# Moving a substitution tile's clears and eleven weight remainders from GpSimd to VectorE in a hybrid decoder step

## The chip, the cores and the metric

The kernel runs on one core of a Trainium2 chip. The metric is the device time of one execution in microseconds (us); the median of three runs is given. Five engines of the core work beside each other, each through its own instructions in a fixed order: TensorE (PE in the profile, with its weight loads as PEld), VectorE (DVE), ScalarE (ACT), GpSimd (POOL) and SyncE (SP), which issues the transfers.

## The reference

One inference step of a hybrid decoder layer for 2048 prompt tokens and 8 x 8 sample tokens, model width 1024. Cut to what matters here:

```python
h = _rmsnorm(x, norm_mix_w[i]) * (1 + sc1) + sh1
proj = jnp.einsum('bld,de->ble', h, w_in[i])
qkv, z, b_raw, a_raw, sq, sk, sv = _split_cols(proj, IN_SPLITS)
o_dn, n_dn_buf, n_S = _deltanet_mixer(qkv, z, b_raw, a_raw, ...)   # 4 heads, chunks of 64
o_swa, n_k, n_v = _swa_prompt(sq, sk, sv, swa_sinks[i], rel_bias)  # window 128
mix = jnp.concatenate([o_dn, o_swa], axis=-1)
x = x + g1 * jnp.einsum('ble,ed->bld', mix, w_out[i])
h = _rmsnorm(x, norm_ffn_w[i]) * (1 + sc2) + sh2
u = jnp.einsum('bld,df->blf', h, ffn_w_up[i])
gate, up = jnp.split(u_c + ffn_conv_b[i], 2, axis=-1)              # u_c: causal convolution of u
x = x + g2 * jnp.einsum('blf,fd->bld', jax.nn.silu(gate) * up, ffn_w_down[i])
```

In each chunk the DeltaNet mixer needs the inverse of a unit lower triangular matrix:

```python
A = jnp.where(strict, bc[..., :, None] * kk * decay, 0.0)
T = lax.linalg.triangular_solve(A + eye, jnp.broadcast_to(eye, A.shape),
                                left_side=True, lower=True, unit_diagonal=True)
```

## The kernel before

**Tiling.** The 2112 tokens lie along the columns, in two halves: HALVES is [512, 512] and [384, 384, 320] columns, and the last 64 columns of the last block are the sample tokens. The half is hf in the code, the block bi. Rows are model features, in 8 tiles of 128 (KT). The input projection has 22 column tiles m, the output projection 8, the up projection 44. The program runs the first half's input projection; then its mixers (DeltaNet and attention, by chunks of 128 tokens: `front` prepares a chunk, later steps use it) interleaved with the second half's input projection; the first half's output projection (`between`); its up projection interleaved with the second half's mixers; the second half's output projection and up projection; and the down projection.

**Weights as two parts.** Every matmul is made of three products of rounded high and low parts. `load_split` (tile `w_raw`, two buffers) loads 128 x 1024 weights; `split` has ScalarE round them (`w_hi`, L368) and another engine subtract (`w_lo` = w_raw - w_hi, L369). `gemm_steps` issues the three products (L377) for each of the eight k: w_hi with the high part of the input, w_hi with the low part, w_lo with the high part. Which engine makes w_lo is chosen by the caller: VectorE unless told otherwise. In the second half, `inproj` gives odd m to GpSimd, and `out_weights` every other new tile.

**The output projection.** `outproj` runs the 8 feature tiles of a block: 24 matmuls into `op_ps`; a load of the residual tile `xr` (two buffers); `residual` (L1325, VectorE) adds it to the result; a store to x2T; ScalarE squares it and GpSimd adds the squares up (`acc`, L1337). In the block with the sample tokens `x`, `sres` and `x2s` (L1325 to L1329, L1275) take xr's place. Beside it `ffn_in` normalises the block before: TensorE sums the squares over partitions (`ss_ps`), VectorE scales (`rsq`, L144), GpSimd takes the power -1/2 (`rtok`, L145), VectorE lays it on diagonals (`dg`, L230, three of 128 x 128), TensorE spreads these with a matrix of ones (`rb_ps`, L234), and VectorE multiplies (`ht`, L302) and forms low parts (`lo`, L309).

**The substitution.** `front` turns a chunk's matrix (tile G) into an inverse of its 16 x 16 diagonal blocks in the tile `TU`, one buffer: the first half of TU is cleared (L772) and its diagonal set to one (L773), both on GpSimd; VectorE substitutes row by row (L774 to L781), copies the transposed result (L784), and SyncE stores TU to memory (`tu_d`). There are 16 chunks and one front for the sample tokens. TU's clear has to wait for the stores of the front before. Mixed with the fronts run the evacuations of the projections on VectorE (`ev`, `sg`, `cv` at L589 and L1370), the DeltaNet's own (`Kt`, `S`, `vb`, `Y`) and the low parts.

**Early tiles.** `early_h` normalises 15 tiles of the second half's input in spare places before the projection that uses them: a load (`he`), a VectorE and a ScalarE step each.

**The order.** The code is written as generators, which `beside` interleaves by the shares in SHARE; then a scheduler with a cost model orders the instructions of each engine (TileContext with schedule_with_timeline_sim, L2249). So a change of one engine's instruction can move others.

Of the kernel before, what the change touches and what calls it, by code (L numbers as in the profile page):

```python
# [18 lines left out]
AF = mybir.ActivationFunctionType  # L19
ALU = mybir.AluOpType  # L20
# [5 lines left out]
KT = 8  # L26
# [11 lines left out]
HALVES = [[(0, 512), (512, 512)], [(1024, 384), (1408, 384), (1792, 320)]]  # L38
# [8 lines left out]
BS = 16  # L47
# [48 lines left out]
def kernel(  # L96
# [5 lines left out]
    nc = tc.nc  # L102
# [35 lines left out]
    MOD = cp.tile([P, 6, KT, 9], F32, tag="MOD", name="MOD")  # L138
# [102 lines left out]
    def h_tile(hf, bi):  # L241

        c0, n = HALVES[hf][bi]
        a = KT * (c0 - HALVES[hf][0][0])
        return [t[:, a:a + KT * n].rearrange("p (k n) -> p k n", k=KT) for t in h_at]

    made = {}

    def early_h(pool):


        def spare(tag, bufs=1, size=1):
            t = pool.tile([P, 4 * size, P], F32, tag=tag, name="he", bufs=bufs).rearrange("p h i -> p (h i)")
            return [t[:, 512 * i:512 * i + 512] for i in range(size)]

        room = iter(spare("xz") + spare("qs", 1, 2) + spare("kh") + spare("kl") + spare("u") + spare("o")
                    + spare("nl", 3) + spare("nl", 3) + spare("nl", 3) + [spare(t, 2)[0] for t in ("pt", "pt", "PT", "PT")] + spare("he"))
        for i, t in enumerate(room):
            bi, k = divmod(i, KT)
            c0, n = HALVES[1][bi]  # L260
            t = made[bi, k] = t[:, :n]
            nc.sync.dma_start(t, I["xT"][k, :, c0:c0 + n])
            nc.vector.scalar_tensor_tensor(t, t, MOD[:, 1, k, 0:1], rB_tile(1, bi), ALU.mult, ALU.mult)
            nc.scalar.activation(t, t, AF.Identity, bias=MOD[:, 0, k, 0:1], scale=1.0)
            yield True

    def affine_h(hb, bi, hf, branch, rB, src, ks=range(KT), pool_too=lambda k: k % 2, smp=None):
# [84 lines left out]
    def rB_tile(hf, bi):  # L352
        c0, n = HALVES[hf][bi]
        a = c0 - HALVES[hf][0][0]
        return sg_at[0][:, a:a + n]


    def load_raw(src):
        raw = gw.tile([P, KT, P], F32, tag="w_raw", name="w_raw", bufs=2)
        loads.append(nc.sync.dma_start(raw, src).ins)  # L360
        return raw

    def load_split(src, eng=None, out=None):
        return split(load_raw(src), eng, out)

    def split(raw, eng=None, out=None):
        hi, lo = out or [gw.tile([P, KT, P], F32R, tag=t, name=t, bufs=2) for t in ("w_hi", "w_lo")]
        nc.scalar.copy(hi, raw)  # L368
        (eng or nc.vector).tensor_tensor(lo, raw, hi.bitcast(F32), ALU.subtract)  # L369
        return hi, lo  # L370

    def gemm_steps(ps, w, hb, n, ks=range(KT), first=None, last=None):

        (wh, wl), (hh, hl) = w, hb
        for k in ks:
            for i, (a, b) in enumerate(((wh, hh), (wh, hl), (wl, hh))):
                nc.tensor.matmul(ps[:, :n], a[:, k, :], b[:, k, :n],  # L377
                                 start=first is not False and k == ks[0] and i == 0,
                                 stop=last is not False and k == ks[-1] and i == 2)
            yield True  # L380
# [29 lines left out]
    def project(ms, src, load, hb, hf, evac, after=None, freed=None, tags=("acc",), turn=(2, 2), third=None, w0=None):  # L410


        order = list(pairs(ms, turn, len(HALVES[hf])))
        new = [m for i, (m, _) in enumerate(order) if m not in [x for x, _ in order[:i]]]
        first = max(2, turn[0])
        w = {m: w0 if w0 and not i else (load, third)[i == 2](m) for i, m in enumerate(new[:first])}
        new = new[first:]
        last = {bi: i for i, (_, bi) in enumerate(order)}
        for i, (m, bi) in enumerate(order):
            ps = bank(src, tags[i % len(tags)])  # L420
            yield from gemm_steps(ps, w[m], hb[bi], HALVES[hf][bi][1])
            end = bi == len(HALVES[hf]) - 1
            if end and new:
                w[new[0]] = load(new[0])
                new.pop(0)
            evac(m, bi, ps)
            if end and after:
                after(m)
            if freed and last[bi] == i:
                freed(bi)  # L430
# [5 lines left out]
    def pairs(ms, turn, nb):  # L436


        ms = list(ms)
        a, b = turn[0], len(ms) - turn[1]  # L440
        for g in [ms[:a]] + [[m] for m in ms[a:b]] + [ms[b:]]:
            for bi in range(nb):
                for m in g:
                    yield m, bi
# [187 lines left out]
    def in_evac(hf, bi, m, ps, ic):  # L632
        c0, n = HALVES[hf][bi]
        np_ = n - LS if c0 + n == LT else n
        ev = evp[0].tile([P, 512], F32, tag="cv", name="ev", bufs=evp[2])[:, :n]
        if m < 12:
            o = ic["out"]
            rb = conv_block(ps, n, np_, o[:, m, 0:3], b8(o[:, m, 3:27]), ic["cw"][:, m], None, ev)
            if TWICE[hf] == 2:
                silu2(ev, rb)  # L640
            else:
                nc.scalar.activation(ev, ev, AF.Silu)
        elif m < 16:
            nc.scalar.activation(ev, ps[:, :n], AF.Tanh, scale=0.5)
            nc.vector.scalar_tensor_tensor(ev, ev, 1.0, ps[:, :n], ALU.add, ALU.mult)  # L645
            nc.gpsimd.tensor_scalar(ev, ev, ic["dnw"], 1.0, ALU.mult, ALU.mult)
        elif m < 20:
            nc.scalar.mul(ev, ps[:, :n], -0.125)
        else:
            nc.scalar.copy(ev, ps[:, :n])  # L650
        nc.sync.dma_start(proj[m, :, c0:c0 + n], ev)
        if m in range(16, 21):
            lo = evp[0].tile([P, 512], F32R, tag="cv", name="ev_lo", bufs=evp[2])[:, :np_]
            nc.scalar.copy(lo, ev[:, :np_])
            nc.vector.tensor_tensor(lo.bitcast(F32), ev[:, :np_], lo.bitcast(F32), ALU.subtract)
            nc.sync.dma_start(low_d[m - 16, :, c0:c0 + np_], lo.bitcast(F32))
        if m == 20 and c0 + n == LT:
            nc.sync.dma_start(O["p_swa_k"], ev[:, np_ - P:np_])
            nc.sync.dma_start(O["s_swa_k_new"], ev[:, np_:])

    def inproj(hf, h, ic, ms, **kw):
        return project(ms, "in_ps", lambda m: load_split(I["w_inT"][m], nc.gpsimd if hf and m % 2 else nc.vector), h, hf,
                       lambda m, bi, ps: in_evac(hf, bi, m, ps, ic), **kw)


# [4 lines left out]
    def bank(name, tag):  # L670
        return pm.tile([P, 512], F32, tag=tag, name=name, bufs=BANKS[tag])
# [19 lines left out]
    def front(c, d, pool, rows=P):  # L691
        c0 = P * c
# [76 lines left out]
        yield True  # L769
        TU = pool.tile([4 * P // BS, 2, BS, BS], F32, tag="TU", name="TU", bufs=1)  # L770
        T0 = TU[:np_, 0]
        nc.gpsimd.memset(T0, 0.0)  # L772
        nc.gpsimd.memset(T0.rearrange("p i j -> p (i j)")[:, ::BS + 1], 1.0)  # L773
        nc.vector.tensor_scalar_mul(T0[:, 1:, 0], G[:np_, 0, 1:], -1.0)  # L774
        for j in range(1, BS - 1):
            shape = [np_, BS - 1 - j, j + 1]
# [297 lines left out]
    def sample_delta(sp):  # L1074
        d = {}
        S0 = sp.tile([P, NB_S, H, P], F32, tag="S0", name="S0")
        nc.sync.dma_start(S0, I["state_ssm"].rearrange("p (b h) d -> p b h d", b=NB_S))
        yield from front(NCH, d, sp, LS)


# [160 lines left out]
    def out_weights(hf):  # L1241

        seq = [m for o in OUT_ORDER[:len(HALVES[hf])] for m in o]
        w = {m: load_split(I["w_outT"][m]) for m in seq[:2]}
        for i, m in enumerate(seq):
            yield w[m]
            if m not in seq[i + 1:i + 3]:
                del w[m]
                new = next((x for x in seq[i + 1:] if x not in w), None)
                if new is not None:  # L1250
                    w[new] = load_split(I["w_outT"][new], nc.gpsimd if hf and i % 2 else None)
            yield

    def outproj(hf, bi, mix, sums, op, weights, kept=None):
# [204 lines left out]
    class Quarters:  # L1459
# [26 lines left out]
        def load(self, p, i):  # L1486
            if p < MI:
                loads.append(nc.sync.dma_start(self.raws[i], I["w_upT"][2 * p + 1 - i]).ins)
# [474 lines left out]
    with ExitStack() as main:  # L1963
# [12 lines left out]
        with ExitStack() as es:  # L1976
            ps0 = new_pool(es, "ps0", space=PSUM)
            bank0 = lambda name: ps0.tile([P, 512], F32, tag="a", name=name, bufs=2)
            with ExitStack() as es0:
# [27 lines left out]
                h = [h_tile(0, bi) for bi in range(2)]  # L2007
# [62 lines left out]
        def ahead(hf, pool):  # L2070
            c0 = NCH // 2 * hf
            ds = chunks
            yield from front(c0, ds[c0], pool)
            yield from lockstep(levels(ds[c0], pool), front(c0 + 1, ds[c0 + 1], pool))
# [55 lines left out]
        with ExitStack() as es:  # L2130
            up_tags[:] = FREE_TAGS
            filler, h = between(1, filler, es, range(2 * PLAIN))
# [120 lines left out]
```

## Time and profile before

| what | value |
|---|---|
| median of three runs | 2581.04 us (2580.18 to 2581.7) |
| the profiled execution | 2575.84 us, span 2574.1 us, granted clock 0.996 |
| busy: TensorE, its weight loads | 2512.2 us, 2208.6 us |
| busy: VectorE, ScalarE, GpSimd | 1804.9, 1284.1, 780.7 us |
| w_lo on VectorE, on GpSimd | 106 and 20 of them |
| clears of TU on GpSimd | 17 of 32 x 256 (one of 16 x 256), 17 of the diagonal |

Busy times are sums over the whole span; the granted clock is the share of full speed that TensorE was given. A row of the waits names who waited, for whom, how long in total, how many times, and the longest. Rows of the timeline have the start, the duration, the engine, the line and the operation with its output and inputs, and in brackets the idle time before it and what ended that; a row with xN stands for N instructions in a run. A row of the windows has the busy time and the count of each engine in a stretch, then the granted clock, the share of the transfer engines and the GB/s.

### The profile page before, as it was taken

The numbers are of one execution on the slowest core, as the hardware profiler recorded it, in microseconds if no ns is written. First come the engines' busy times: TensorE is split into PE (matmuls) and PEld (weight loads), VectorE is DVE, ScalarE is ACT, GpSimd is POOL, SyncE is SP. The second block draws the span as 40 slices with busy tenths as digits, with TensorE's granted clock in tenths as the row PEclk, the third lists the DMA queues.
The fourth block names the chain that finished last, engine by engine and source line by source line (L and its number), as shares of the span: only waits on it lengthen the run. The fifth ranks groups of instructions, "written<-read, shape, count | busy, mean of one in ns | idle before, by whom it ended". The sixth has DMA issues, their size and how long they took to land.

```text
span 2574.1 us, 45295 instructions
## 1 busy us (share of the span) xinstructions
PE 2512.2 (98%) x16410; PEld 2208.6 (86%) x16410; DVE 1804.9 (70%) x3616; ACT 1284.1 (50%) x3131; POOL 780.7 (30%) x702
## 2 busy tenths in 40 slices
PE   7999999999999999999999999999999999999998
PEld 5777888988988787888877789999999998888998
DVE  6466488887534687887758665886777676686676
ACT  5554365564443555555543353655555554454453
POOL 2064142333233222221111144355555520022012
PEclk9999999999999999999999999999999999999999
DMA  7887454433466443433355376324555458676463
GB/s 279 279 302 249 140 140 112 119 105 110 117 205 200 136 112 85 122 105 95 88 170 189 114 246 196 102 96 149 173 175 184 169 173 288 215 242 206 132 194 131
DMA packets 315852, 427.62 MB, mean 166 GB/s; under 512 B 82243, under 2 KB 206244, under 8 KB 315364
## 3 DMA queue, kind: packets, MB, share of 16 engines
q1 hardware_dynamic: 315052, 423.55, 52.0%
q8 instruction: 129, 2.11, 0.4%
q0 software_dynamic: 288, 1.11, 0.1%
q14 instruction: 95, 0.78, 0.1%
q10 hardware_dynamic: 288, 0.06, 0.0%
HBM read 305.07 MB, written 120.57 MB: 165 GB/s over the span
## 4 chain that ended last, share of the span: by engine, by line
PE 73%; DVE 11%; DMA 7%; ACT 3%; issue 3%; POOL 2%; SPq 1%; POOLq 0%; DVEq 0%; ACTq 0%
PE dn_ps L1871 17%; PE up_ps L377 16%; PE in_ps L377 9%; PE uq_b L1653 6%; PE op_ps L377 5%; PE uq_c L1653 3%; DVE ev L589 3%; PE uq_u L1653 2%; PE uq_g L1653 2%; PE uq_a L1653 1%; DMA wada<-in_w_ada_dram 1%; PE as_ps L1016 1%; PE pv_ps L1054 1%; DMA mt<-mixd 1%; DVE w_lo L369 1%
## 5 line engine op out<-in xcount | busy, mean ns | idle before, releaser
L377 PE MATMUL in_ps<-hi,w_hi 128*128 128x512 f32 (+2 forms) x880 | 317.9, 364 | 7.7 <-DVE ev L645 2.7
L377 PE MATMUL in_ps<-lo,w_hi 128*128 128x512 f32 (+2 forms) x880 | 314.8, 358 | 2.6 <-DVE lo L309 1.5
L377 PE MATMUL in_ps<-hi,w_lo 128*128 128x512 f32 (+2 forms) x880 | 313.0, 356 | 1.5 <-POOL w_lo L369 1.5
L377 PE MATMUL up_ps<-hi,w_hi 128*128 128x512 f32 (+2 forms) x808 | 312.9, 388 | 0.0
L377 PE MATMUL up_ps<-hi,w_lo 128*128 128x512 f32 (+2 forms) x808 | 311.7, 387 | 0.0
L377 PE MATMUL up_ps<-lo,w_hi 128*128 128x512 f32 (+2 forms) x808 | 311.2, 386 | 0.0
L1871 PE MATMUL dn_ps<-tl,wh 128*128 128x512 f32 (+2 forms) x796 | 271.7, 342 | 0.0
L1871 PE MATMUL dn_ps<-th,wh 128*128 128x512 f32 (+2 forms) x796 | 269.9, 341 | 0.0
L1871 PE MATMUL dn_ps<-th,wl 128*128 128x512 f32 (+2 forms) x796 | 269.3, 341 | 0.0
L368 ACT CAST w_hi<-w_raw 128x1024 fp32r<-128x1024 f32 x126 | 132.0, 1048 | 144.1 <-PE op_ps L377 53.3
L369 DVE TENSOR_TENSOR w_lo<-w_raw,w_hi 128x1024 fp32r<-128x1024 f32 x106 | 133.8, 1262 | 84.1 <-ACT w_hi L368 78.3
L377 PEld LDWEIGHTS in_ps<-hi,w_hi 128*128 128x128 f32 x880 | 164.9, 188 | 27.7 <-DVE ev L645 3.1
L377 PEld LDWEIGHTS in_ps<-lo,w_hi 128*128 128x128 f32 x880 | 165.6, 188 | 22.4 <-issue 3.6
L377 PEld LDWEIGHTS up_ps<-hi,w_lo 128*128 128x128 f32 x808 | 151.7, 188 | 35.1 <-issue 9.1
L377 PEld LDWEIGHTS in_ps<-hi,w_lo 128*128 128x128 f32 x880 | 165.4, 188 | 17.9 <-POOL w_lo L369 1.8
L377 PEld LDWEIGHTS up_ps<-hi,w_hi 128*128 128x128 f32 x808 | 151.9, 188 | 29.4 <-issue 3.5
L377 PEld LDWEIGHTS up_ps<-lo,w_hi 128*128 128x128 f32 x808 | 151.9, 188 | 27.7 <-issue 2.7
L1755 ACT CAST wh<-wr 128x512 fp32r<-128x512 f32 x149 | 92.2, 620 | 154.6 <-PE dn_ps L1871 103.2
L1871 PEld LDWEIGHTS dn_ps<-tl,wh 128*128 128x128 f32 x796 | 150.5, 189 | 15.9 <-DVE tl L1756 0.6
L1871 PEld LDWEIGHTS dn_ps<-th,wl 128*128 128x128 f32 x796 | 150.5, 189 | 15.2
L1871 PEld LDWEIGHTS dn_ps<-th,wh 128*128 128x128 f32 x796 | 150.2, 189 | 15.5
L589 DVE SCALAR_TENSOR_TENSOR ev<-rb,cw,ev 128x512 f32<-128x512 f32 (+2 forms) x180 | 138.8, 776 | 33.9 <-ACT ev L582 32.0
(574 smaller groups left out, 6441.9 us busy)
## 6 DMA issues: line engine op xcount, KB each, us to landing
w_raw<-in_w_upT_dram SPq DMA_DIRECT2D x50, 512.0 KB
wada<-in_w_ada_dram SPq DMA_DIRECT2D x48, 512.0 KB
w_raw<-in_w_inT_dram SPq DMA_DIRECT2D x44, 512.0 KB
wr<-ws_d SPq DMA_DIRECT2D x88, 256.0 KB
w_raw<-in_w_outT_dram SPq DMA_DIRECT2D x34, 512.0 KB
d<-act_d SPq DMA_DIRECT2D x33, 512.0 KB
wr<-in_w_downT_dram SPq DMA_DIRECT2D x66, 256.0 KB
proj<-ev SPq DMA_DIRECT2D x44, 256.0 KB
```

The lines of the kernel that those rows point to most:

```text
L368: nc.scalar.copy(hi, raw)
L369: (eng or nc.vector).tensor_tensor(lo, raw, hi.bitcast(F32), ALU.subtract)
L377: nc.tensor.matmul(ps[:, :n], a[:, k, :], b[:, k, :n], start=first is not False and k == ks[0] and i == 0, stop=last is not False and k == ...
L589: nc.vector.scalar_tensor_tensor(out, src(j), w[:, j:j + 1], out, ALU.mult, ALU.add)
L1016: nc.tensor.matmul(banks[v][:, 256 * g:256 * g + 256 - P * k0], qs[:, 2 * (g0 + g) + v], t[:, v, :2 - k0].rearrange("p w j -> p (w j)"), s ...
L1054: mm = nc.tensor.matmul(pv_ps[64 * v:64 * v + 64, :], (vprev[0], vt if k0 else dv)[half][:, 64 * v:64 * v + 64], PT[v, half], start=half = ...
L1653: nc.tensor.matmul(bk[t][:, :nb], u[:, k], v[:, k], start=new and k == 0 and y == 0, stop=k == KG - 1 and y == 2, skip_group_check=True)
L1755: nc.scalar.copy(h, raw)
L1871: nc.tensor.matmul(acc[m, s][:, :n], w[q, i][a][:, c], th[b][:, v], start=new and i == 0 and y == 0, stop=i == KH - 1 and y == 2, skip_gro ...
```

## The change

Four edits. (1) `early_h` asks for each input tile three steps before the steps that use it. (2) In `inproj` the low parts of m = 19 and 21 in the second half go from GpSimd to VectorE. (3) In `out_weights` all low parts are VectorE's; nine of the second half's had been GpSimd's. (4) In `front` both clears of TU are VectorE's, 34 memsets. GpSimd keeps nine of its 20 low parts.

```diff
@@ early_h
     made = {}
+    EARLY = 3
...
-        for i, t in enumerate(room):
-            bi, k = divmod(i, KT)
-            c0, n = HALVES[1][bi]
-            t = made[bi, k] = t[:, :n]
-            nc.sync.dma_start(t, I["xT"][k, :, c0:c0 + n])
-            nc.vector.scalar_tensor_tensor(t, t, MOD[:, 1, k, 0:1], rB_tile(1, bi), ALU.mult, ALU.mult)
-            nc.scalar.activation(t, t, AF.Identity, bias=MOD[:, 0, k, 0:1], scale=1.0)
+        left = []
+        for i, t in enumerate([*room, *[None] * EARLY]):
+            if t is not None:
+                bi, k = divmod(i, KT)
+                c0, n = HALVES[1][bi]
+                t = made[bi, k] = t[:, :n]
+                nc.sync.dma_start(t, I["xT"][k, :, c0:c0 + n])
+                left.append((bi, k, t))
+            if i >= EARLY:
+                bi, k, t = left.pop(0)
+                nc.vector.scalar_tensor_tensor(t, t, MOD[:, 1, k, 0:1], rB_tile(1, bi), ALU.mult, ALU.mult)
+                nc.scalar.activation(t, t, AF.Identity, bias=MOD[:, 0, k, 0:1], scale=1.0)
             yield True
@@ inproj
-        return project(ms, "in_ps", lambda m: load_split(I["w_inT"][m], nc.gpsimd if hf and m % 2 else nc.vector), h, hf,
+        return project(ms, "in_ps", lambda m: load_split(I["w_inT"][m], nc.gpsimd if hf and m % 2 and m < 18 else nc.vector), h, hf,
@@ front
-        nc.gpsimd.memset(T0, 0.0)
-        nc.gpsimd.memset(T0.rearrange("p i j -> p (i j)")[:, ::BS + 1], 1.0)
+        nc.vector.memset(T0, 0.0)
+        nc.vector.memset(T0.rearrange("p i j -> p (i j)")[:, ::BS + 1], 1.0)
@@ out_weights
-                    w[new] = load_split(I["w_outT"][new], nc.gpsimd if hf and i % 2 else None)
+                    w[new] = load_split(I["w_outT"][new])
```

Line numbers after `early_h` are higher by six in the changed kernel (w_lo is L375, dg stays L230, xr is L1331). How the scheduler then orders the instructions is shown at three places.

VectorE in the second output projection, around the rsq and dg of its first normalised block; before:

```order
L369 TENSOR_TENSOR w_lo<-w_raw,w_hi 128x1024
L1325 SCALAR_TENSOR_TENSOR xr<-op_ps,MOD,xr 128x384 x4
L369 TENSOR_TENSOR w_lo<-w_raw,w_hi 128x1024
L1325 SCALAR_TENSOR_TENSOR xr<-op_ps,MOD,xr 128x384
L144 TENSOR_SCALAR rsq<-ss_ps 128x3
L230 TENSOR_SCALAR dg<-cst,rtok 128x128 x3
L1325 SCALAR_TENSOR_TENSOR xr<-op_ps,MOD,xr 128x384
L369 TENSOR_TENSOR w_lo<-w_raw,w_hi 128x1024
L302 SCALAR_TENSOR_TENSOR ht<-ht,MOD,rb_ps 128x384 x5
L309 SCALAR_TENSOR_TENSOR lo<-ht,MOD,hi 128x384 x2
```

The same place after:

```order
L1331 SCALAR_TENSOR_TENSOR xr<-op_ps,MOD,xr 128x384
L375 TENSOR_TENSOR w_lo<-w_raw,w_hi 128x1024
L1331 SCALAR_TENSOR_TENSOR xr<-op_ps,MOD,xr 128x384 x3
L375 TENSOR_TENSOR w_lo<-w_raw,w_hi 128x1024
L144 TENSOR_SCALAR rsq<-ss_ps 128x3
L230 TENSOR_SCALAR dg<-cst,rtok 128x128 x3
L1331 SCALAR_TENSOR_TENSOR xr<-op_ps,MOD,xr 128x384
L375 TENSOR_TENSOR w_lo<-w_raw,w_hi 128x1024
L308 SCALAR_TENSOR_TENSOR ht<-ht,MOD,rb_ps 128x384 x5
L1331 SCALAR_TENSOR_TENSOR xr<-op_ps,MOD,xr 128x384
L375 TENSOR_TENSOR w_lo<-w_raw,w_hi 128x1024
```

The rsq and the three dg now stand right behind a w_lo, one xr sooner than before, and a w_lo follows nearly every xr.

ScalarE at the last column tile of the second half's input projection, where mixh are casts of the first mixer outputs for the output projection; before:

```order
L1231 CAST mixh<-mt 128x512 x3
L368 CAST w_hi<-w_raw 128x1024
L648 ACTIVATE ev<-in_ps 128x320
L1231 CAST mixh<-mt 128x512
L654 CAST ev_lo<-ev 128x256
```

After:

```order
L660 CAST ev_lo<-ev 128x384
L1237 CAST mixh<-mt 128x512
L374 CAST w_hi<-w_raw 128x1024
L654 ACTIVATE ev<-in_ps 128x320
L1237 CAST mixh<-mt 128x512
L660 CAST ev_lo<-ev 128x256
```

The cast w_hi of that tile stands behind one mixh instead of three.

VectorE in a mixer of the second half, beside the up projection of the first half, after the substitution of one front (the COPY of TU is its last step, and the stores of TU follow it on SyncE); before:

```order
L781 TENSOR_TENSOR TU<-TU,gt 32x15
L784 COPY TU<-TU 32x256
L589 SCALAR_TENSOR_TENSOR cv<-rb,fcw,cv 128x512 x2
L1370 SCALAR_TENSOR_TENSOR cv<-cv,sg 128x512
L728 TENSOR_TENSOR Kt<-kq_ps_12976,bn 128x512
L922 SCALAR_TENSOR_TENSOR S<-S,cdec,s_ps 128x128 x4
```

After:

```order
L787 TENSOR_TENSOR TU<-TU,gt 32x15
L790 COPY TU<-TU 32x256
L595 SCALAR_TENSOR_TENSOR cv<-rb,fcw,cv 128x512 x2
L778 MEMSET TU 32x256
L1376 SCALAR_TENSOR_TENSOR cv<-cv,sg 128x512
L779 MEMSET TU 32x16
L734 TENSOR_TENSOR Kt<-kq_ps_12976,bn 128x512
L928 SCALAR_TENSOR_TENSOR S<-S,cdec,s_ps 128x128 x4
```

The clear of TU for the next front stands right behind the two cv, ahead of the third cv, Kt and S, and waits there for the stores.

SyncE's loads of the early tiles (he) stand in the same order before:

```order
L701 DMA xv<-proj 128x4x128
L262 DMA he<-in_xT_dram 128x384 x2
L651 DMA proj<-ev 128x512
L262 DMA he<-in_xT_dram 128x384 x8
L360 DMA w_raw<-in_w_inT_dram 128x1024
```

and after:

```order
L707 DMA xv<-proj 128x4x128
L265 DMA he<-in_xT_dram 128x384 x2
L657 DMA proj<-ev 128x512
L265 DMA he<-in_xT_dram 128x384 x8
L366 DMA w_raw<-in_w_inT_dram 128x1024
```

Only the line numbers differ there.

## The prediction

> **What bounds the kernel now.** I read first the page's row of busy times, then the waits of TensorE, then three stretches: the second output projection, the end of the second input projection, and the mixers. All times are of the one profiled execution: span 2574.1 us, time 2575.84 us, which lies 5.2 us under the median of the runs shown (2581.04). The sum is made against 2575.84, and its difference is then taken off the median.
>
> ```profile
> PE 2512.2 (98%) x16410; PEld 2208.6 (86%) x16410; DVE 1804.9 (70%) x3616; ACT 1284.1 (50%) x3131; POOL 780.7 (30%) x702
> ```
>
> TensorE is busy for 98% of the span, so 61.9 us are its idle time, and no edit here takes a matmul away. VectorE's 70% is an average; what counts is where TensorE waits for it.
>
> ```profile
> PE rb_ps L234 <- DVE dg L230: 6.4, 5, 3.3
> PE op_ps L377 <- DVE w_lo L369: 3.3, 2, 2.6
> PE in_ps L377 <- POOL w_lo L369: 1.5, 1, 1.5
> PE op_ps L377 <- POOL w_lo L369: 1.4, 3, 0.6
> ```
>
> The columns are us in total, times, and the longest. Only the last two rows, 2.9 us, are waits for a low part that GpSimd makes. The change can also act through the first two, because dg and the VectorE low parts run beside GpSimd's:
>
> ```profile
> 1551.94 1.22 DVE L369 TENSOR_TENSOR w_lo<-w_raw,w_hi 128x1024 fp32r<-128x1024 f32 x1
> 1558.29 0.62 DVE L1325 SCALAR_TENSOR_TENSOR xr<-op_ps,MOD,xr 128x384 f32<-128x384 f32 x1 [5.13 <-DMA xr<-in_xT_dram]
> 1558.82 0.15 DVE L144 TENSOR_SCALAR rsq<-ss_ps 128x3 f32<-128x3 f32 x1
> 1559.94 3.51 DVE L230 TENSOR_SCALAR dg<-cst,rtok 128x128 f32<-128x128 f32 x3 [0.97 <-POOL rtok L145]
> 1630.40 0.68 DVE L230 TENSOR_SCALAR dg<-cst,rtok 128x128 f32<-128x128 f32 x3 [0.97 <-POOL rtok L145]
> ...
> 1559.05 0.86 POOL L145 TENSOR_TENSOR rtok<-rsq,mhalf 128x3 f32<-128x3 f32 x1 [8.65 <-DVE rsq L144]
> 1559.88 2.35 POOL L369 TENSOR_TENSOR w_lo<-w_raw,w_hi 128x1024 fp32r<-128x1024 f32 x1
> ```
>
> Columns: start, us, engine, line, operation, and in brackets the idle time before and what ended it. The same three dg took 0.68 us at 1630.40 and 3.51 us at 1559.94, where GpSimd's w_lo began 0.06 us earlier and ran 2.35 us. They also began late: rsq stood in VectorE's queue behind an xr whose load landed only at 1558.3. TensorE's side of it:
>
> ```profile
> 1558.66 0.34 PE L377 MATMUL op_ps<-mixh,w_hi 128*128 128x384 f32 x1
> 1558.84 0.34 PE L377 MATMUL op_ps<-mixl,w_hi 128*128 128x384 f32 x1
> 1562.46 2.08 PE L234 MATMUL rb_ps<-dg,ones 128*128 128x128 f32 x6 [3.28 <-DVE dg L230]
> 1564.19 0.67 PE L377 MATMUL op_ps<-mixh,w_lo 128*128 128x384 f32 x1
> ...
> 1568.82 0.40 PE L377 MATMUL op_ps<-mixl,w_hi 128*128 128x384 f32 x1
> ...
> 1540.00:1580.00 40.00, 36.63 (x195) 36.04 (x194) 21.48 (x27) 17.13 (x28) 19.44 (x15) 0.91 0.68 213
> 1580.00:1626.00 46.00, 41.99 (x268) 40.60 (x267) 33.90 (x55) 19.16 (x32) 27.62 (x20) 1.00 0.55 181
> ```
>
> Matmuls start 0.18 us apart before the gap. After it, 14 steps from 1564.19 to 1568.82 take 4.63 us, 0.33 each, and the window's granted clock (third column from the end) is 0.91 instead of 1.00. So the gap costs 3.28, then 14 x 0.18 = 2.52 becomes 4.63 (2.1 lost), and the six rb_ps matmuls at about half speed lose half of their 2.08 (1.0): together 6.4 us. That is the largest single price the change touches.
>
> **The change part by part.**
>
> Input tiles asked for sooner. The issue order on SyncE has the same he loads in the same places before and after, and VectorE and ScalarE show the same rows there. Only the bookkeeping of the loop moves, not an instruction, so the price is 0 with both ends at 0.
>
> Low parts of the second output projection: nine move.
>
> ```profile
> L369 DVE TENSOR_TENSOR w_lo<-w_raw,w_hi x106: 1201/1224/2294, 14.8 to 1675.8; 128x1024 fp32r<-128x1024 f32 x106
> L369 POOL TENSOR_TENSOR w_lo<-w_raw,w_hi x20: 2346/2396/2710, 341.8 to 1615.9; 128x1024 fp32r<-128x1024 f32 x20
> ```
>
> Minimum, median, maximum in ns. Each costs VectorE 1.22 us where it cost GpSimd 2.40. In the first block of 384 columns the new order has rsq and the dg ahead of the xr that waits, right after the w_lo that ended at 1553.2, and no GpSimd w_lo beside them: 1553.2 + 0.15 + 0.97 for rtok + 0.68 is 1555, or 1556 if the sums come a little later. TensorE wants them at 1559, so the 6.4 us go. What is late next: each w_lo now stands behind an xr waiting for its load. The load that lands at 1558.3 does so whatever VectorE does, so the w_lo behind it ends at 1558.29 + 0.62 + 1.22 = 1560.1, and TensorE, without its gap, wants it at about 1559.1: 1.0 us. Walking on through the block in this way gives 0.3, 0.1, 1.0 and 0.35 more: 2.8 in all, an estimate. Gain 6.4 - 2.8 = 3.6 us; ends 0 and 6.4. TensorE also waited 0.24 us at 1532.8 for a GpSimd low part; that goes.
>
> The second block, 320 columns:
>
> ```profile
> 1607.97 0.41 PE L377 MATMUL op_ps<-mixh,w_lo 128*128 128x320 f32 x1 [0.58 <-POOL w_lo L369]
> 1614.33 0.41 PE L377 MATMUL op_ps<-mixh,w_lo 128*128 128x320 f32 x1 [2.58 <-DVE w_lo L369]
> 1618.70 0.41 PE L377 MATMUL op_ps<-mixh,w_lo 128*128 128x320 f32 x1 [0.58 <-POOL w_lo L369]
> 1596.33 3.44 DVE L230 TENSOR_SCALAR dg<-cst,rtok 128x128 f32<-128x128 f32 x3 [0.58 <-POOL rtok L145]
> ```
>
> TensorE waits 3.7 us here. VectorE was busy for 33.90 of these 46 us. Four low parts add 4 x 1.22 = 4.9 us to it; the dg lose their hold (3.44 - 0.68 = 2.8 us), and two or three other pairs of overlapping instructions about as much again, 5.5 in all. So VectorE's load stays as it was, its waits turn from GpSimd's into its own, and I take a gain of 0.7 (ends: loss 2.5, gain 3.7). Sum for this projection 3.6 + 0.24 + 0.7 = 4.5 us.
>
> GpSimd's remaining adds (L1337) can in turn hold a w_lo on VectorE: its longest, 2294 ns, is 1070 over the median, and the mean of the 106 is 1262, 38 ns over it. Eleven moved parts at 38 ns make 0.4 us, most of it off the path; I take 0. The Trainium skill, "SBUF — State Buffer", section "SBUF: two separate sides", states that a VectorE operation with two SBUF inputs and a GpSimd operation that reads SBUF exclude each other for the whole instruction, which speaks against giving VectorE more such operations. The dg row agrees with a hold of a full GpSimd instruction; by that rule at its worst each of the eleven would pay the 1.07 of the maximum, 11.8 us of VectorE time, and the gain of this part would be gone.
>
> Low parts of the last input tiles: two move.
>
> ```profile
> 731.12 1.05 ACT L368 CAST w_hi<-w_raw 128x1024 fp32r<-128x1024 f32 x1
> 732.25 2.53 POOL L369 TENSOR_TENSOR w_lo<-w_raw,w_hi 128x1024 fp32r<-128x1024 f32 x1 [0.25 <-ACT w_hi L368]
> 734.83 0.44 PE L377 MATMUL in_ps<-hi,w_lo 128*128 128x384 f32 x1 [1.51 <-POOL w_lo L369]
> ```
>
> ScalarE's order now puts w_hi after one mixh cast instead of three, and VectorE needs 1.2 instead of 2.53 us: even with w_hi still ending at 732.17, the low part is there at 732.17 + 1.22 = 733.4, and TensorE first wants it at 734.83 - 1.51 = 733.3. Two casts fewer ahead bring it under that. Ends: 0, if TensorE, being earlier, waits for the next transfer instead; 2.5, if GpSimd's mixl, which then need not wait out the w_lo, ends a later wait too. I take 1.5.
>
> The clears: 34 memsets move to VectorE.
>
> ```profile
> L772 POOL MEMSET TU<- x17: 301/302/303, 228.6 to 1330.3; 32x256 f32 x16, 16x256 f32 x1
> L773 POOL MEMSET TU<- x17: 114/116/118, 229.0 to 1330.6; 32x16 f32 x16, 16x16 f32 x1
> L1023 DVE MEMSET nl<- x4: 272/272/272, 331.9 to 332.7; 128x256 f32 x4
> POOL TU L772 <- DMA tu_d<-TU: 71.8, 12, 22.4
> ```
>
> VectorE's nearest memset of 256 columns took 272 ns, also beside GpSimd's work; with 116 for the small one, 17 x 0.39 = 6.6 us of VectorE time. The last row is the rub: twelve of the clears waited for the stores that read TU, 71.8 us in all. GpSimd could wait; on VectorE everything behind waits too, evacuations (cv, sg, ev), Kt and w_lo. How long depends on the slot in the order. One of the worst:
>
> ```profile
> 1162.25 1.52 DVE L589 SCALAR_TENSOR_TENSOR cv<-rb,fcw,cv 128x512 f32<-128x512 f32 x2
> 1163.81 0.69 DVE L1370 SCALAR_TENSOR_TENSOR cv<-cv,sg 128x512 f32<-128x512 f32 x1
> 1166.28 0.69 DVE L728 TENSOR_TENSOR Kt<-kq_ps,bn 128x512 f32<-128x512 f32 x1 [1.78 <-PE s_ps L916]
> ...
> 1166.45 0.30 POOL L772 MEMSET TU<- 32x256 f32 x1 [5.62 <-DMA tu_d<-TU]
> 1166.81 0.12 POOL L773 MEMSET TU<- 32x16 f32 x1
> ```
>
> In the new order the clear stands between the two cv at 1163.8, and its stores land at about 1166.4: 2.6 us of hold, of which VectorE was idle 1.78, so Kt comes about 1.2 us late. Laid beside the order in this way, some ten of the seventeen slots come before their landing, by 0 to 2.6 us; at 1.3 on average, 13 us. With the clears themselves, VectorE loses some 20 us spread over 1100 us. What covers it, in the stretch where eight of the fronts lie:
>
> ```profile
> PE up_ps L377 <- ACT sg L584: 1.5, 1, 1.5
> PE o_ps L908 <- DVE vb L903: 0.5, 1, 0.5
> ...
> 1000.00:1300.00 300.00, 298.99 (x2312) 239.72 (x2310) 242.93 (x681) 161.03 (x504) 69.33 (x62) 1.00 0.38 102
> ```
>
> TensorE waited for VectorE once for 0.5 us from 860 to 1300, and VectorE has 57 of 300 us idle. Most of the hold falls there. I take 1.5 us on the path, one hold's overhang (1.2) and a little; ends: 0, and 8, where 40% of the 20 comes through. GpSimd loses 17 x 0.42 = 7.1 us of clears and 11 x 2.40 = 26.4 us of low parts, none of it behind a wait of TensorE except those counted.
>
> Sum: -4.5 - 1.5 + 1.5 = -4.5: 2575.84 becomes 2571.3, and the median 2576.5.
>
> **The rivals.**
>
> VectorE becomes the bound in the second output projection. For it: 33.90 of 46 us busy, and every w_lo behind an xr with a wait like 5.13. Then the 1.0 and 0.35 of the walk grow until block one gains nothing beyond the 1 us, block two loses 2, and with the clears' 1.5 the time is about 2580.5. Against: dg is certainly earlier.
>
> The clears hold up the mixers, and the kernel is slower. Place: the fronts, price 20 us of VectorE time. It decides when a hold outlasts the idle time and buffers behind it: a hold of 2.6 against 1.78 idle does already. If two thirds of it reach TensorE, 13.5 less the 6 of the other parts is +7.5: 2588.5. From 11 us, a little over half, it is slower by more than 0.2%. Against it is the 0.5 us in 440.
>
> All of it comes: the 6.4, the 0.24, the 3.7 and the 1.5 vanish, and the clears cost nothing: -11.8, so 2569.2. Against: the load landing at 1558.3 doesn't move by itself.
>
> That the change doesn't do what it says holds for the early tiles, and is in the sum; the order shows the other parts done.
>
> **How the numbers follow.** The forecast case, 0.48, has its own range 2572 to 2580 around 2576.5; VectorE as the bound 0.22 at 2580.5; slower 0.15; all of it 0.15. About 0.2%, 5.2 us, is what a measurement can tell from no change: under 2575.9 is faster, over 2586.2 slower. The fourth case and about half of the first give 0.39 for faster; the third, mostly, and a little of the second give 0.14 for slower; the rest, 0.47, is no difference. The range 2569 to 2584 leaves out the slower case and a part of the fourth.
>
> **What would show it.** At the second output projection: three dg of about 0.7 us, no rb_ps wait above 1 us, granted clock 1.00 where it was 0.91, waits of op_ps for VectorE's w_lo of 0.3 to 1 us. The wait at 734.8 gone. TU memsets on VectorE with waits for tu_d of 10 to 15 us in all, and few new waits of TensorE for VectorE between 225 and 1330. It would be wrong if those waits add up to over 5 us, if op_ps waits for w_lo by more than 7 us, or if the reordered instructions elsewhere open a gap over 3 us that halves the clock.

## The result and the profile after

The changed kernel took 2570.28 us, the median of 11 runs, beside 2577.44 us for the kernel before in 11 runs of its own. The ratio is 0.9967, 95% interval 0.9957 to 0.9977: 8.5 us less (5.9 to 11.1). The median lies within the forecast range, and the sign is right, but the forecast of 4.5 us less was about half of it and lies outside the interval. What the prediction held likeliest, no difference within 5.2 us (0.47), did not come; faster had 0.39. The forecast time of 2576.5 had been reckoned from a median of 2581.04; from the 2577.44 measured here, the same 4.5 us less is 2572.9. All ratios here are of undisturbed executions: one of 7330.43 us, of the kernel with the clears put back, is left out.

The profiled execution of the changed kernel is one of its slower ones: 2573.88 us, span 2572.1, 2.0 us under the span before. A second profiled execution of the same kernel (called the second trace below) has a span of 2559.1. So the two traces have to be read together, and neither alone gives the size. First the page's busy times and the waits of TensorE in the first trace, in the columns of the prediction:

```profile
PE 2509.4 (98%) x16410; PEld 2207.0 (86%) x16410; DVE 1805.8 (70%) x3661; ACT 1283.7 (50%) x3131; POOL 750.4 (29%) x657
PE op_ps L383 <- DVE w_lo L375: 4.4, 4, 2.0
PE rb_ps L234 <- DVE dg L230: 3.8, 3, 2.2
```

GpSimd lost 30 us of work, VectorE's sum stayed (1804.9 before): its low parts take 13.1 us more and the clears 5.8, but others take less, among them dg 4.6, lo 3.4 and x2s 2.1. That all of these had been held by GpSimd's operations is shown for dg alone (below). TensorE waits 2.6 us less for dg, 1.1 us more for VectorE's low parts, and not at all for GpSimd's. VectorE at the first normalised block of the second output projection, in the first trace:

```profile
1553.24 1.22 DVE L375 TENSOR_TENSOR w_lo<-w_raw,w_hi 128x1024 fp32r<-128x1024 f32 x1
1555.20 0.16 DVE L144 TENSOR_SCALAR rsq<-ss_ps 128x3 f32<-128x3 f32 x1 [0.74 <-PE ss_ps L225]
1556.34 0.68 DVE L230 TENSOR_SCALAR dg<-cst,rtok 128x128 f32<-128x128 f32 x3 [0.97 <-POOL rtok L145]
1559.86 0.62 DVE L1331 SCALAR_TENSOR_TENSOR xr<-op_ps,MOD,xr 128x384 f32<-128x384 f32 x1 [2.84 <-DMA x<-in_xT_dram]
1560.40 1.22 DVE L375 TENSOR_TENSOR w_lo<-w_raw,w_hi 128x1024 fp32r<-128x1024 f32 x1
```

The three dg take 0.68 us, and TensorE's wait of 3.28 us for them is gone. A new wait stands 15 us later. TensorE, then VectorE, then the windows of the same trace:

```profile
1577.06 0.44 PE L383 MATMUL op_ps<-mixh,w_lo 128*128 128x384 f32 x1 [2.00 <-DVE w_lo L375]
...
1572.48 0.62 DVE L308 SCALAR_TENSOR_TENSOR ht<-ht,MOD,rb_ps 128x384 f32<-128x384 f32 x1 [2.26 <-DMA ht<-x2T]
1575.13 1.88 DVE L375 TENSOR_TENSOR w_lo<-w_raw,w_hi 128x1024 fp32r<-128x1024 f32 x1
...
1579.00:1581.00 2.00, 2.00 (x8) 2.00 (x7) 1.24 (x1) 0.44 (x1) 1.58 (x2) 0.50 0.96 372
1540.00:1580.00 40.00, 38.01 (x215) 37.28 (x214) 23.01 (x32) 17.52 (x28) 15.83 (x13) 0.98 0.76 236
1580.00:1626.00 46.00, 44.40 (x284) 43.74 (x283) 33.41 (x63) 22.24 (x36) 19.14 (x15) 0.98 0.60 188
```

A w_lo stood behind an ht that waited 2.26 us for its load, then took 1.88 us; TensorE waited 2.00 us and ran at half clock (0.50) afterwards. In the second trace the same two windows, and TensorE's two waits for a low part in the projection, are:

```profile
1540.00:1580.00 40.00, 39.82 (x235) 39.50 (x235) 23.84 (x35) 18.04 (x29) 16.19 (x13) 1.00 0.69 219
1580.00:1626.00 46.00, 44.66 (x290) 44.10 (x289) 40.22 (x77) 27.90 (x54) 19.43 (x15) 1.00 0.53 171
1562.70 0.44 PE L383 MATMUL op_ps<-mixh,w_lo 128*128 128x384 f32 x1 [0.18 <-DVE w_lo L375]
1599.61 0.41 PE L383 MATMUL op_ps<-mixh,w_lo 128*128 128x320 f32 x1 [1.34 <-DVE w_lo L375]
```

There the long wait and the half clock are absent. (The second trace is 5.8 us ahead of before at 1540, 12.1 at 1580 and 15.7 at 1626, so its second window reaches into the work after the projection, and its 40.22 us of VectorE can't be set beside 33.90. Over the matmuls that before ran from 1580 to 1626, VectorE is busy for 32.1 us in it.) To see where time comes and goes, the table lays each trace beside the trace of before, matmul by matmul (the same name and ordinal): by how many us the shift changes over a stretch, medians over 21 matmuls at its ends. Negative is a gain. Stretches are by the clock of before; the last four columns are experiments told below.

| stretch of before, us | first trace | second trace | output part alone | input part alone | clears alone | clears on GpSimd again (2nd) |
|---|---|---|---|---|---|---|
| 0 to 220 | -0.3 | 0.5 | 2.7 | 1.9 | -0.6 | 0.9 |
| 220 to 728, mixers | 1.0 | -1.6 | -2.1 | 1.0 | -1.5 | -0.1 |
| 728 to 764, end of input projection | -3.7 | -3.2 | -1.2 | -3.0 | 0.2 | -2.2 |
| 945 to 1100, mixers | 4.8 | -0.5 | -0.5 | 2.1 | -0.3 | -0.5 |
| 1515 to 1553 | -1.1 | -1.1 | -0.7 | 1.0 | 1.2 | -1.0 |
| 1553 to 1572, dg | -6.5 | -6.7 | -5.5 | -2.4 | -1.0 | -6.7 |
| 1572 to 1590 | 3.9 | 0.4 | 1.2 | 0.0 | 0.0 | 0.7 |
| 1590 to 1640 | -3.2 | -3.6 | -3.2 | 0.0 | 0.0 | -3.5 |
| 1640 to 1720 | 1.3 | 1.3 | 1.3 | 0.0 | 0.0 | 1.3 |
| end, all together | -1.5 | -15.0 | -4.2 | 0.4 | -0.5 | -7.2 |

What repeats in every column with an edit, and only there, belongs to the edit; the rest are draws, differences between executions by chance. Before 220 us, where none of the edits has changed an instruction's work, the columns already differ by 3.3 us.

### The profile page after: what moved, and what is told of

It reads as the page before. It is cut to its first block, busy times and chain, and to the rows that moved or that the text cites. A ratio compares the mean times of both kernels' runs of the same rounds, so it can differ in the third digit from the quotient of the medians.

```text
span 2572.1 us, 45289 instructions
## 1 busy us (share of the span) xinstructions
PE 2509.4 (98%) x16410; PEld 2207.0 (86%) x16410; DVE 1805.8 (70%) x3661; ACT 1283.7 (50%) x3131; POOL 750.4 (29%) x657
## 4 chain that ended last, share of the span: by engine, by line
PE 67%; DVE 13%; DMA 10%; issue 3%; ACT 3%; POOL 2%; SPq 1%; DVEq 0%; POOLq 0%; ACTq 0%
PE dn_ps L1877 17%; PE up_ps L383 14%; PE in_ps L383 9%; PE uq_b L1659 5%; PE op_ps L383 5%; PE uq_c L1659 2%; PE uq_u L1659 2%; DVE ev L595 2%; PE uq_g L1659 2%; PE uq_a L1659 1%; DMA wada<-in_w_ada_dram 1%; DMA mt<-mixd 1%; PE pv_ps L1060 1%; DMA qs<-low_d 1%; DMA suv<-in_w_downT_dram 1%
## 5 line engine op out<-in xcount | busy, mean ns | idle before, releaser
L375 DVE TENSOR_TENSOR w_lo<-w_raw,w_hi 128x1024 fp32r<-128x1024 f32 x117 | 146.9, 1256 | 72.3 <-ACT w_hi L374 71.0
```

## The experiments

Each kernel was timed beside the kernel before. Us are the ratio times the median of before in that comparison.

**The parts alone.** Of the second output projection, only this:

```diff
-                    w[new] = load_split(I["w_outT"][new], nc.gpsimd if hf and i % 2 else None)
+                    w[new] = load_split(I["w_outT"][new])
```

> The kernel before with one edit: all low parts of the second output projection made by VectorE. The prediction's sum gave 4.5 us less for this part (2576.5 against 2581.0). The trace of the changed kernel, with its matmuls laid beside those of before one by one, gains 7.0 us between 1518 and 1640: by it 7 us less. Rival: VectorE is the bound there and all is given back, 0 to 1 us less. In the profile: no wait of rb_ps for dg over 1 us around 1560, and no half clock after it.

Ratio 0.9974 (0.9961 to 0.9986): 6.7 us less (3.6 to 10.1). It agrees with the trace's reading of 7, and the prediction's 4.5 is inside the interval too; "all given back" is out.

Of the input projection, only this:

```diff
-        return project(ms, "in_ps", lambda m: load_split(I["w_inT"][m], nc.gpsimd if hf and m % 2 else nc.vector), h, hf,
+        return project(ms, "in_ps", lambda m: load_split(I["w_inT"][m], nc.gpsimd if hf and m % 2 and m < 18 else nc.vector), h, hf,
```

> The kernel before with one edit: the low parts of m = 19 and 21 of the second half's input projection made by VectorE. The prediction gave 1.5 us less. The trace of the changed kernel gains 3.5 us from 728 to 757 (1.7 at the wait for the low part, 1.9 at the waits that followed it up to the first op_ps): by it 3.5 us less. Rival: the mixd loads set the end and the gain is given back by 757, 0.

Ratio 0.9989 (0.9976 to 1.0001): 2.8 us less (6.2 less to 0.3 more). The wait of 1.51 us for GpSimd's low part is gone from its trace; here is VectorE there:

```profile
732.78 1.23 DVE L369 TENSOR_TENSOR w_lo<-w_raw,w_hi 128x1024 fp32r<-128x1024 f32 x1 [0.20 <-DMA low_d<-ev_lo]
```

The stretch 728 to 764 gains 3.0 us, but kernels without this edit also came out there between 1.8 us better and 0.2 worse. The mean of the nine traces with the edit is 2.1 us better than that of the five without.

Of the clears, only the two memsets of `front` on VectorE:

```diff
-        nc.gpsimd.memset(T0, 0.0)
-        nc.gpsimd.memset(T0.rearrange("p i j -> p (i j)")[:, ::BS + 1], 1.0)
+        nc.vector.memset(T0, 0.0)
+        nc.vector.memset(T0.rearrange("p i j -> p (i j)")[:, ::BS + 1], 1.0)
```

> The kernel before with one edit: the 34 clears of TU on VectorE. The prediction gave 1.5 us more (0 to 8). The trace of the changed kernel loses 4.9 us from 945 to 1100 and about 1.5 between 560 and 660, at waits for VectorE's and ScalarE's steps in the mixers: by it 5 to 6 us more. Rival: the order that the scheduler makes from the clears is the cause of the gain that the other parts don't explain, then 2 to 4 us less. In the profile: waits of TU's clear for tu_d on VectorE of about 20 us in all.

Ratio 1.0008 (0.9997 to 1.0018): 2.1 us more (0.8 less to 4.6 more). Neither 5 to 6 us more nor a gain of 2 to 4. The three parts add up to 6.7 + 2.8 - 2.1 = 7.4 us less, beside 8.5 (5.9 to 11.1) measured together: no unexplained part is needed, though the intervals would hide one of a few us. The early tiles alone were not run; their instructions stand in the same order.

The clears of the changed kernel put back on GpSimd, in two comparisons:

```diff
-        nc.vector.memset(T0, 0.0)
-        nc.vector.memset(T0.rearrange("p i j -> p (i j)")[:, ::BS + 1], 1.0)
+        nc.gpsimd.memset(T0, 0.0)
+        nc.gpsimd.memset(T0.rearrange("p i j -> p (i j)")[:, ::BS + 1], 1.0)
```

> The changed kernel with the clears of TU back on GpSimd. If the clears cost what the changed kernel's trace shows, it is 5 us faster than the changed kernel, about 13 us less than before by the times (8.5 + 5); if the prediction's 1.5 us holds, 10 us less; if the clears bring the unexplained part of the gain, it is slower than the changed kernel, 5 to 6 us less than before.

> The changed kernel with the clears back on GpSimd, again. The clears alone measured +2.1 us; so this should be 2 us faster than the changed kernel run beside it. If the prediction's hold on VectorE is larger than that, 4 us or more; if it is hidden, the same time.

Ratio 0.9964 (0.9954 to 0.9974) and 0.9954 (0.9942 to 0.9967): 9.3 and 11.9 us less. The changed kernel run again beside the second one:

> The changed kernel again, beside the three kernels below and with a second profile. If the 4.9 us that its first trace lost between 945 and 1100 belong to the change, they stand in this trace too, and the parts' sum by time (6.7 + 2.8 - 2.1 = 7.4 us less) is short by them; if half of them were a draw of that execution, the losses there are under 2.5 us here. Time 7 to 9 us less than before.

Ratio 0.9964 (0.9951 to 0.9978), 9.3 us less. So without the clears' move the kernel is perhaps 2.6 us better than the changed one (medians 2565.70 and 2568.26), but the intervals overlap, and in the first comparison its ratio was 0.9964, beside 0.9967 for the changed kernel: whether this version beats both is not settled. The loss of 4.8 us from 945 to 1100 was a draw: the three other traces with the clears on VectorE and one buffer show a gain of 0.3 and 0.5 and a loss of 0.8 there. Of TensorE's waits there, the three longest in the first trace, then the only one in the second (940 to 1300):

```profile
PE z_ps L832 <- DMA T<-tu_d: 1.2, 1, 1.2
PE z_ps L832 <- DVE T L855: 1.1, 1, 1.1
PE p_ps L907 <- DVE xz L965: 1.1, 1, 1.1
```

```profile
PE o_ps L914 <- DVE vb L909: 0.7, 1, 0.7
```

**Hold or queue place?** A hold is here the time by which an operation runs longer beside one of GpSimd's than alone. At the dg, two things changed at once: no GpSimd low part beside them, and rsq ahead of the xr that waits. One kernel has the first alone (to before, i = 9 counts the steps of `out_weights`):

```diff
-                    w[new] = load_split(I["w_outT"][new], nc.gpsimd if hf and i % 2 else None)
+                    w[new] = load_split(I["w_outT"][new], nc.gpsimd if hf and i % 2 and i != 9 else None)
```

> The kernel before with one low part moved: of the second output projection's nine, only the fourth (i = 9, the one that GpSimd began at 1559.88 beside the dg) goes to VectorE. In the order rsq stays behind the same xr, so dg isn't earlier, but nothing of GpSimd's two-input work runs beside it. If the hold of dg by that one low part is what costs 6.4 us, the wait of rb_ps falls from 3.28 to under 1 us, the clock isn't halved, and the kernel is about 5 us faster. If the late rsq is the cause, the wait stays at 2 to 3 us and the time as before.

Ratio 0.9984 (0.9973 to 0.9995): 4.1 us less. Its VectorE and TensorE:

```profile
1560.07 0.62 DVE L1325 SCALAR_TENSOR_TENSOR xr<-op_ps,MOD,xr 128x384 f32<-128x384 f32 x1 [4.56 <-DMA xr<-in_xT_dram]
1560.60 0.15 DVE L144 TENSOR_SCALAR rsq<-ss_ps 128x3 f32<-128x3 f32 x1
1562.64 1.41 DVE L230 TENSOR_SCALAR dg<-cst,rtok 128x128 f32<-128x128 f32 x3 [0.75 <-POOL rtok L145]
1563.80 0.91 PE L234 MATMUL rb_ps<-dg,ones 128*128 128x128 f32 x6 [0.89 <-DVE dg L230]
```

rsq still stands behind the xr that waits, but dg take 1.41 instead of 3.51 us (a GpSimd add, acc, of 0.99 us runs beside them from 1562.58), TensorE waits 0.89 instead of 3.28, and the six rb_ps run in 0.91 us instead of 2.08: full clock. The counterpart has all but that one low part on VectorE:

```diff
-                    w[new] = load_split(I["w_outT"][new], nc.gpsimd if hf and i % 2 else None)
+                    w[new] = load_split(I["w_outT"][new], nc.gpsimd if hf and i == 9 else None)
```

> The counterpart: the nine low parts on VectorE except the one with i = 9, which stays on GpSimd. In the order rsq now stands ahead of the xr that waits, so the dg can begin some 3 us sooner, beside that low part. If the hold is the cause, dg still take 3.5 us, rb_ps waits 1 us or more and at most half of the 6.7 us that all nine gave is left; if the place of rsq in the queue is the cause, the wait is under 0.5 us and the kernel is 5 to 7 us faster than before.

Ratio 0.997 (0.9955 to 0.9985): 7.7 us less. Its VectorE, GpSimd and TensorE:

```profile
1553.41 0.16 DVE L144 TENSOR_SCALAR rsq<-ss_ps 128x3 f32<-128x3 f32 x1 [1.12 <-PE ss_ps L225]
1554.54 0.68 DVE L230 TENSOR_SCALAR dg<-cst,rtok 128x128 f32<-128x128 f32 x3 [0.97 <-POOL rtok L145]
1555.47 0.62 DVE L1325 SCALAR_TENSOR_TENSOR xr<-op_ps,MOD,xr 128x384 f32<-128x384 f32 x1 [0.25 <-DMA xr<-in_xT_dram]
...
1555.70 2.40 POOL L369 TENSOR_TENSOR w_lo<-w_raw,w_hi 128x1024 fp32r<-128x1024 f32 x1 [1.19 <-ACT w_hi L368]
...
1558.25 0.83 PE L234 MATMUL rb_ps<-dg,ones 128*128 128x128 f32 x6
```

I had expected the dg to run beside that low part. They don't: with rsq early they end at 1555.2, before its w_hi is there. So it is a chain: the late rsq is what puts the dg beside the low part, which then holds them. Either cure takes most of it; the earlier rsq takes all, 6.7 us in the table's stretch against 4.5 in the trace of the one moved part.

**The new wait at 1577.** One low part back to GpSimd, and the clears too, in two comparisons:

```diff
-        nc.vector.memset(T0, 0.0)
-        nc.vector.memset(T0.rearrange("p i j -> p (i j)")[:, ::BS + 1], 1.0)
+        nc.gpsimd.memset(T0, 0.0)
+        nc.gpsimd.memset(T0.rearrange("p i j -> p (i j)")[:, ::BS + 1], 1.0)
...
-                    w[new] = load_split(I["w_outT"][new])
+                    w[new] = load_split(I["w_outT"][new], nc.gpsimd if hf and i == 12 else None)
```

> The changed kernel with the clears back on GpSimd, and one low part, i = 12, given to GpSimd. That one ended the wait of 2.00 us at 1577 after which the clock was halved for 3.3 us (3.8 us together): on VectorE it stood behind an ht that waited 2.3 us for its load. If that place in the queue is the cause, the wait and the half clock go, 3.8 us less than with all on VectorE (2569.3 in its runs): about 2565.5, 13 us less than before. If GpSimd's low part then holds VectorE's lo and ht instead, another wait of 1 to 2 us comes and the time is 2568 to 2570.

> The same with the low part i = 12 on GpSimd, again, beside the kernel without it. The traces differ by 3.8 us at 1577 (a wait of 2.00 and a half clock of 3.4 us). If the half clock follows that wait in every execution, 3.8 us faster than the kernel with all nine on VectorE; if it follows only in some, between 2 and 3.8; if the wait itself is a draw, 0 to 1.

Ratio 0.9963 (0.9952 to 0.9974) and 0.9967 (0.9955 to 0.9979). The kernel with the clears on GpSimd and all nine on VectorE has 0.9954 beside the second and had 0.9964 in its first comparison: no gain, and the 13 us expected at first are missed. Of the seven traces with all nine on VectorE, two have the wait of 2.00 us; in the others the waits near there are 0.17 to 1.06. So its size was a draw, and the wrong thing to mend. The first trace puts it down to the landing of the load of ht; in the other trace with it (the clears put back, first comparison), loads of ht (1.41 us) and xr (1.31 us) held VectorE one after the other.

**The hold of the clears.** Two buffers for the cleared part of TU (in the second half's fronts):

```diff
-        TU = pool.tile([4 * P // BS, 2, BS, BS], F32, tag="TU", name="TU", bufs=1)
-        T0 = TU[:np_, 0]
+        TU = [pool.tile([4 * P // BS, BS, BS], F32, tag=t, name=t, bufs=2 if t == "TU" and NCH // 2 <= c < NCH else 1)
+              for t in ("TU", "TV")]
+        T0 = TU[0][:np_]
...
```

> The changed kernel with TU in two tiles and two buffers of the part that is cleared, for the second half's eight fronts: their clears needn't wait for the stores of the front before. VectorE's clears stay. If the hold by the stores (19.8 us of waits on VectorE, more than half of it there) is what the clears cost, this is 1.5 to 3 us faster than the changed kernel, 10 to 11.5 us less than before, and no clear waits for tu_d after 900; if the hold is hidden, the same time as the changed kernel, 8.5 less.

The copy and the stores (left out here) use the two tiles accordingly. Ratio 0.9985 (0.9971 to 0.9998), 3.9 us less than before: slower than the changed kernel, if anything, and why is open. Its waits of the clears, beside the first trace's:

```profile
DVE TU L779 <- DMA tu_d<-TU: 18.8, 10, 3.0
```

```profile
DVE TU L778 <- DMA tu_d<-TU: 19.8, 9, 4.2
```

The edit didn't take the waits away: the scheduler used the second buffer to place each clear a front earlier, again right behind a substitution whose stores it must wait for. One clear, for instance, waits 2.64 us from 1117.5 for the stores of the substitution whose copy ended at 1116.5. The run tells nothing of the hold. The other try makes the clear wait for G:

```diff
-        nc.vector.memset(T0, 0.0)
+        nc.vector.tensor_scalar_mul(T0, G[:np_], 0.0)
```

> The changed kernel with TU's first clear replaced by a VectorE product of G and zero, so that it stands behind the load of G, where the substitution has to wait anyway, and no longer behind the stores of the front before. The work stays on VectorE. If the hold by the stores is what the clears cost, the waits for tu_d (19.8 us) go and the time is that of the kernel with clears on GpSimd, 2 us under the changed kernel; if the 17 operations themselves cost, it is as the changed kernel; if the longer chain of the front reaches TensorE, 1 to 4 us slower than it.

Ratio 0.9969 (0.9957 to 0.9981), medians 2569.43 and 2568.26 for the changed kernel beside it. The waits for tu_d are gone, replaced by waits for G:

```profile
DVE TU L778 <- DMA G<-at_d: 16.8, 8, 4.6
```

The time is that of the changed kernel. Either the hold was hidden, or the later substitution gave back what it brought; the run doesn't tell these apart.

## Why the prediction was right or wrong

The sign and the mechanism at the dg were right; the size was not, and with it the likeliest outcome, no difference, which rested on a gain under 5.2 us. The step that failed is the sum for the second output projection, put at 4.5 us: the traces show 6.7, and so does the run with that part alone, though its interval (3.6 to 10.1) holds both. Within the sum the term furthest off is the second block, taken as 0.7 and found as 3.2 to 3.6: it let VectorE's waits take the place of GpSimd's, which they did not. The input part was also under-sized. Term by term:

- **The gap at the dg**: right in mechanism. The prediction priced it at 6.4 us; the traces gain 6.5 and 6.7 from 1553 to 1572. The price was, however, that of one execution: in two kernels in which nothing changed there, the same place came out 2.4 and 1.0 us cheaper, because TensorE waited 2.3 and 2.2 us there. The mean of the three is about 1.1 us less than the price.
- **The wait at 1532.8**: mis-sized, 0.24 us forecast. It was the luckiest of three executions: in the kernels with only the input part or only the clears changed, TensorE waited 1.6 and 1.8 us for GpSimd's low parts from 1515 to 1553. In the traces with the output part it does not wait for them at all.
- **The walk through the first block**: mis-sized. It took five waits of 2.8 us in all, the first from a load that lands at 1558.3 "whatever VectorE does". It isn't fixed: in the kernel with i = 9 kept the load ended its wait at 1555.5, and the second trace has one wait, of 0.18 us, where the first has 2.00 and a half clock. The stretch 1572 to 1590 loses 0.4 to 1.8 in five of the seven traces with all nine on VectorE, and 3.9 and 4.3 in the two with the wait of 2.00.
- **The second block**: mis-sized, 0.7 us forecast, 3.2 to 3.6 found. VectorE's load stayed nearly as forecast (33.41 beside 33.90 in the first trace, over the same matmuls 32.5), but its waits didn't take over GpSimd's: both waits of 0.58 vanished, and 2.58 became 1.34. A balance of busy time said nothing on which operation ends last.
- **What follows it**: not foreseen. 1.3 us (0.7 in one) are given back in the seven traces with all nine on VectorE, at one place in the up projection of the second half, where VectorE in six of them waits 1.89 or 1.90 us for a load (act_d), for which it did not wait before. TensorE in the first trace:

```profile
1699.27 0.45 PE L1659 MATMUL uq_a<-hi,rl 128*128 128x384 f32 x1 [1.12 <-DVE rl L1515]
```

- So the output part, as the mean of those seven traces against the mean of the three in which GpSimd has all nine, is 1.5 (1515 to 1553) + 5.0 (dg) - 2.0 (1572 to 1590) + 3.4 (second block) - 1.2 (what follows) = 6.7, against 4.5. That it meets the 6.7 of the run to the tenth is luck: single traces differ by nearly 4 us in one of these stretches.
- **The input part**: right in mechanism, 1.5 forecast, 2.8 measured with a wide interval, 2.1 by the traces. A later wait of TensorE in the trace of before was not in the term:

```profile
751.80 0.41 PE L377 MATMUL in_ps<-hi,w_hi 128*128 128x320 f32 x1 [1.03 <-ACT ev L650]
```

  It is gone in the first trace, and 0.41 us of it is left in the kernel with the input part alone. But the four other kernels that leave the input part as it was have 0 to 0.44 us there too, so the 1.03 was a draw of one execution, not a gain of the edit.
- **The clears**: forecast 1.5 more, measured 2.1 more (0.8 less to 4.6 more), which is told neither from 0 nor from the forecast. The 13 us of waits for the stores were 19.8 and 16.0 in the two traces of the changed kernel. That VectorE's idle time covers most of them fits: TensorE waits once, 0.7 us, from 940 to 1300 in the second trace.
- **The early tiles**: 0, as the order showed; not measured alone.
- **The rivals**: VectorE as the bound of the output projection, and the slower case, are out; "all of it", 11.8 us less, lies just outside the interval (5.9 to 11.1). The time of the first was also added up wrongly: 1 gained and 2 lost in the projection, 1.5 gained at the input and 1.5 lost to the clears make 2582, not 2580.5. The chance of 0.39 for faster was too low. Much of the error came from pricing small waits off the landings of one execution.

## What to carry to other kernels

Where two engines exclude each other, look for what brought the two operations together: here a late rsq put the dg beside a low part, and an earlier place in the queue cured it as well as moving the low part did. Price a gap by several executions, since the wait and the clock after it both vary. A clear that must wait for stores can stand on a busy in-order engine if TensorE has results ahead, but it is no gain there.

## What the runs showed of the hardware

After idle time of TensorE the clock can fall to 0.50 for 3.4 us, which costs 1.7 us. In the 14 traces of this case, from 40 us on and without the last wait of each, 20 of 27 idle times of 1.7 to 2.7 us were followed by it (one of 2.23 us by 6.8 us), and 3 of 78 of 1.2 to 1.65 us; the 3.28 us of before by 6.8. Waits of 2.58 us kept the full clock in the traces of before, of the input part and of the clears; one of 2.57 us at the same place, in the kernel with one low part moved, did not.

What decides, as far as these traces show, is where the idle time falls. Within each trace, all stretches of half clock begin whole multiples of 3.413 us apart. With a trace cut into windows on that grid, half clock followed none of 3061 full-clock windows in which TensorE was idle for under 1.4 us, 1 of 38 with 1.4 to 1.6 us, 7 of 19 with 1.6 to 1.8, and all 18 with more (roughly, since the ends of matmuls are modelled). The wait of 2.58 us in before is spread over two such windows; most of the 2.57 us lies in one. Two windows each of before, then of the kernel with one low part moved; the first figure after the comma is TensorE's busy time, and the clock is third from the end:

```profile
1609.90:1613.31 3.41, 1.86 (x13) 1.59 (x11) 3.41 (x8) 1.69 (x3) 1.12 (x2) 1.00 0.74 252
1613.31:1616.73 3.42, 2.40 (x16) 2.40 (x17) 3.42 (x5) 2.04 (x4) 3.10 (x3) 1.00 0.61 183
```

```profile
1609.93:1613.34 3.41, 1.18 (x8) 1.18 (x9) 3.41 (x6) 2.84 (x5) 1.87 (x2) 1.00 0.69 190
1613.34:1616.75 3.41, 3.41 (x15) 3.41 (x14) 3.38 (x6) 0.72 (x2) 3.12 (x2) 0.50 0.39 136
```

So whether a wait of about 2 us costs the clock is a draw of how it falls on the grid. The Trainium skill, "TensorE: Matmul & The Clock Gate", section "Why this matters for your kernels", asks for no gaps over about 3 us; here 1.7 was enough to lose the clock in most cases.
